# First attention of a two-layer trunk: a head's four score-reading operations emitted with nothing between them

## The chip, the cores and the metric

The kernel runs on one core of a Trainium2 chip. The metric is the device time of one execution in microseconds (us), as the median over several runs. The profile is of one further execution of the same program; its times are counted from the first instruction of its span.

## The reference: what is computed

The reference is a small decoder trunk over one sequence of 256 tokens of width 1024, in float32. It has two layers, and each layer does: a half-step SwiGLU feed-forward, an attention, a second half-step feed-forward. Every sub-layer is fed by an RMS norm that is modulated by a shift and a scale, and its result is added through a gate; shifts, scales and gates are one vector each, made from the conditioning vector `c`:

```python
c_act = silu(c)
mod = c_act @ ada_w[layer] + ada_b[layer]          # 9 vectors of 1024: sh1, sc1, g1, ... sh3, sc3, g3
h = rms_norm(x, g1n) * (1 + sc1) + sh1;  x = x + 0.5 * g1 * swiglu(h, w_in, w_out)
h = rms_norm(x, g2n) * (1 + sc2) + sh2;  x = x + g2 * attention(h)
h = rms_norm(x, g3n) * (1 + sc3) + sh3;  x = x + 0.5 * g3 * swiglu(h, w_in2, w_out2)
```

The first layer's attention is differential: 8 heads, each with two query/key maps of 64 and values of 128 wide. For each of the two maps the logits `q k^T / 8 + bias` go through a causal softmax, the second map's weights are subtracted with a factor lambda, the result multiplies the values, and an RMS norm and an output projection follow. The second layer's attention is an ordinary one with a decay by forget gates. A final RMS norm ends the trunk.

## The kernel before

**Matrix products.** Activations are held as a sum of two lower-precision parts (`HH`, `HL`: 128 features by up to 258 columns for each of eight k), and so are weights (`wh`, `wl`). A product is three matmuls on TensorE: wh·HH, wl·HH, wh·HL (`mm3`, L418). The weights of the whole program are one stream of pieces of mostly 128x1024. Each piece is loaded by SP into one of six buffers (`raw`), rounded by ScalarE (ACT) into its high part `wh` (`cp_part`, L306), and VectorE (DVE) subtracts to get its low half `wl` (`sub_part`, L318). A `raw` buffer comes free, and the next load is issued, when its low half has been made.

**Modulation sums.** The vectors `mod` are not made by TensorE. They are 160 sums on DVE (`ada_block`, L198): each multiplies a 128x1024 tile of `ada_w` with `c_act` and adds it up along the row, which gives 128 numbers of one vector. One load by SP (1 MB) brings a tile for two sums; three such tiles are held, and the load of tile u+3 is issued when the second sum of tile u is done (`ada_dma`, L185). The sums are numbered here from 0: the gate of the first attention and the scale and shift of the feed-forward behind it need the sums up to number 63.

**What sets the order on an engine.** Every instruction of ACT, DVE, TensorE (PE) and SP stays in the order in which the program emits it. While it emits, the program keeps a rough clock for each engine (class `InOrder`, L55). When an instruction would have to wait by these clocks, `fill_dve` (L372) first emits other work ahead of it: low halves, or modulation sums, if the clock of DVE is more than 0.6 us ahead of the operand and a credit allows the sum. The same work is emitted from `bg` (L386), called after each group of matmuls. `plain(f, ...)` (L133) switches the filling off for the time of `f`. In the mode "fill", which starts when the first attention has only its output projection left, `bg` and `fill_dve` emit no sums at all. What is not yet done when a vector is needed is emitted on the spot by `need` (L236), one sum after the other:

```python
def need(*ms):
    while ada_done[0] < 2 * max(ada_at[m] for m in ms):
        credit[0] -= 1
        dve.plainly(ada_block)
```

**The first attention** (`attention_a`, L1050). The heads run as a software pipeline. While PE projects the query/key and value matrices (`v_proj`, `pair_proj`) or multiplies by the output matrix, `group(t)` (L1161) emits for head t the score matmuls and their reading, for head t-1 the transposed weights, for head t-2 the product with the values, for head t-3 the transposed output. The reading is `exps` (L1084): for two maps and two halves of the queries, DVE takes scores plus bias and the row's bound (`nl<-s,g`, 128x128 and 128x256), and ACT takes the exponential. `combine` (L1103) then scales and subtracts the two maps on DVE, `inv_rms` has a power on POOL, and `out_split` makes the high and low part of the head's output (`oh`, `ol`). Until the change, only head 7's reading is emitted through `plain`.

**Behind it.** `OutProj.finish` (L872) emits the last quarter of the output projection into four PSUM banks (`pw`), calls `need` for the gate of this attention and the scale and shift of the next feed-forward, writes the shift into two extra columns of `HH` and `HL` (`shift_cols`, L432), and then, for each of the eight 128-feature blocks n, `x_update` (L438): the residual `x` on DVE, its scaled copy into `HH` on ACT, a square on ACT, the remainder into `HL` on DVE, and a running sum of squares (`acc`) on POOL, the last on DVE. The next feed-forward (`ffn`, kind "late", L632) starts its first product on these not yet normalised columns (`lg`, `lu`), k by k; after k = 2 it issues the matmul of the sum of squares (`psn`, L464), from which the norm is made; its second product (`pg1`) uses the normalised columns.

Of the kernel before, what the change touches and what calls it, by code (L numbers as in the profile page):

```python
# [22 lines left out]
AH = 8  # L23
# [81 lines left out]
def trunk(ctx, tc, a, out):  # L105
# [22 lines left out]
    def bbank(name):  # L128
        return pp.tile([P, 512], F32, tag="tb", name=name)
# [3 lines left out]
    def plain(f, *args):  # L133

        r = []
        act.plainly(lambda: dve.plainly(lambda: r.append(f(*args))))
        return r[0]
# [912 lines left out]
    def attention_a():  # L1050
# [24 lines left out]
        def scores(hd):  # L1075
            sb = [sbank(f"s{hd}_{m}") for m in range(2)]
            for qt, (c0, w) in enumerate(QT):
                for m in range(2):
                    rows = slice(m * HD, m * HD + HD)
                    mm(sb[m][:, c0:c0 + w], qk[hd][rows, qt * P:qt * P + P], qk[hd][rows, 256:256 + w],  # L1080
                       start=True, stop=True)
            return sb

        def exps(hd, sb):  # L1084
            g = gs[hd]
            nl = []
            nm = kp.tile([P, 4], F32, tag="nm", name=f"nm{hd}")
            sm = kp.tile([P, 4], F32, tag="sm", name=f"sm{hd}")
            for m in range(2):
                s = sb[m]  # L1090
                n_ = cp_.tile([P, 384], F32, tag=f"hidh{4 + 2 * (hd % 2) + m}", name=f"nl{hd}_{m}")
                nl.append(n_)
                for qt, (c0, w) in enumerate(QT):
                    cc = 2 * m + qt
                    dve.tensor_tensor_reduce(
                        n_[:, c0:c0 + w], s[:, c0:c0 + w], g[:, S - w:], -0.125, BIG,
                        ALU.add, ALU.min, accum_out=nm[:, cc:cc + 1])
                    act.activation(n_[:, c0:c0 + w], n_[:, c0:c0 + w], AF.Exp,
                                   bias=nm[:, cc:cc + 1], scale=-1.0,
                                   accum_out=sm[:, cc:cc + 1])  # L1100
            st[hd], sms[hd] = nl, sm
# [15 lines left out]
        def weights_t(hd):  # L1117
            pw = abank(f"pw{hd}")
            for b in range(3):
                pe.transpose(pw[:, b * P:b * P + P], st[hd][:, b * P:b * P + P], ident)  # L1120
            return pw

        def values(hd, po):
            wt = st[hd]
            vs = slice((hd % 4) * P, (hd % 4) * P + P)
            v0, v1 = va[0][hd // 4][:, vs], va[1][hd // 4][:, vs]
            mm(po[:, 0:P], wt[:, 0:P], v0, start=True, stop=True)
            mm(po[:, P:2 * P], wt[:, P:2 * P], v0, start=True, stop=False)
            mm(po[:, P:2 * P], wt[:, 2 * P:3 * P], v1, start=False, stop=True)

        def squares(hd, po):
            on = kp.tile([P, 256], F32, tag="w512b", name=f"on{hd}")
            ss = kp.tile([P, 2], F32, tag="ss", name=f"ss{hd}")
            for qt in range(2):
                act.activation(on[:, qt * P:qt * P + P], po[:, qt * P:qt * P + P], AF.Square,
                               accum_out=ss[:, qt:qt + 1])
            st[hd] = (po, on, ss)

        def inv_rms(hd):
            ss = st[hd][2]  # L1140
            dve.tensor_scalar(ss, ss, 1.0 / P, EPS, op0=ALU.mult, op1=ALU.add)
            nc.gpsimd.tensor_tensor(ss, ss, half, op=ALU.pow)
            InOrder.ready[(ss.tensor.name, 0)] = dve.t + 1.0
# [8 lines left out]
        def out_t(hd, pz):  # L1152
            for qt in range(2):
                pe.transpose(pz[:, qt * P:qt * P + P], st[hd][:, qt * P:qt * P + P], ident)

        def out_split(hd, pz):
            oh, ol = o[hd]
            act.activation(oh, pz, AF.Identity, scale=subg)
            dve.scalar_tensor_tensor(ol, pz, subg, oh.bitcast(F32), op0=ALU.mult, op1=ALU.subtract)

        def group(t):  # L1161

            hs, hw, hv, ho = (h if 0 <= h < AH else None for h in (t, t - 1, t - 2, t - 3))
            bank = bbank(f"po{t}") if hv is not None or ho is not None else None
            sb = scores(hs) if hs is not None else None
            pw = weights_t(hw) if hw is not None else None
            if hv is not None:
                values(hv, bank[:, :256])
            if ho is not None:
                out_t(ho, bank[:, 256:])  # L1170
            if hw is not None:
                wt = cp_.tile([P, 384], F32, tag=f"hidh{8 + hw % 2}", name=f"wt{hw}")
                act.copy(wt, pw[:, :384])
                st[hw] = wt
            if hs is not None:
                plain(exps, hs, sb) if hs == AH - 1 else exps(hs, sb)
            if hv is not None:
                squares(hv, bank[:, :256])
                inv_rms(hv)
            if ho is not None:  # L1180
                plain(out_split, ho, bank[:, 256:]) if ho == AH - 1 else out_split(ho, bank[:, 256:])
# [17 lines left out]
        for i, _ in enumerate(v_proj("wv", va)):  # L1199
            run_laters()  # L1200
            if i in (3, 9):
                group(i // 6)
            if i in (5, 11):
                after(i // 6)
        for t in range(2, AH):
            qk.append(qk_tile(t))
            for i, _ in enumerate(pair_proj("wqk", qk[t], f"pqk{t}")):
                if t > 2 and i == 2:
                    group(t - 1)
                if t > 2 and i == 5:  # L1210
                    combine(t - 1)
                if t > 2 and i == 7:
                    scale_o(t - 3)
        step(4)
        group(AH - 1)
        for t, n in (AH - 1, 9), (AH, 6), (AH + 1, 3):
            step(6)
# [362 lines left out]
```

## Time and profile before

| | us |
|---|---|
| median of 3 runs | 966.03 (965.13 to 966.9) |
| the profiled execution | 964.94 |
| its span, first to last instruction | 962.9 |

| engine | busy us | share of the span |
|---|---|---|
| PE | 954.6 | 99% |
| DVE | 821.1 | 85% |
| ACT | 556.9 | 58% |
| POOL | 72.5 | 8% |

PE carries the three matmuls for each product, and its share is near the whole span. A busy PE is not the same as a PE at its peak, since the ends of matmuls are modelled; idle time of PE, however, is seen as such. In the profile almost every operation carries line 100, because a helper records it; the tiles (`ada`, `wl`, `nl`, `pw`, `lg`, ...) tell them apart. A row of the timeline gives start, duration, engine, operation, output and inputs.

The first attention lies between 193 and 301 us of the span, the feed-forward behind it starts at 301.

### The profile page before, as it was taken

How to read it: one execution, taken by the hardware profiler on the slowest of the kernel's cores; microseconds unless marked ns; L12 is line 12 of the kernel's file. 1: busy time of each engine (PE TensorE's matmuls, PEld its weight loads, DVE VectorE, ACT ScalarE, POOL GpSimd, SP SyncE). 2: the span in 40 equal slices, each digit the busy share in tenths (PEclk: the TensorE clock that was granted, in tenths of full speed). 3: DMA queues.
4: the chain of work that ended last, by engine and by line, in shares of the span. 5: the costliest groups of instructions: out<-in, count | busy, mean ns of one | idle time of the engine just before them, and what ended most of it. 6: DMA issues, size and time to landing. Idle time of an engine off the chain costs nothing.

```text
span 962.9 us, 20487 instructions
## 1 busy us (share of the span) xinstructions
PE 954.6 (99%) x8090; PEld 930.9 (97%) x8090; DVE 821.1 (85%) x1369; ACT 556.9 (58%) x908; POOL 72.5 (8%) x119
## 2 busy tenths in 40 slices
PE   9999999999999999999999999999999999999997
PEld 7999999988999999999997999999998899999997
DVE  8989988889999999878889988889988799555575
ACT  6575655566777645455577554445568766554432
POOL 0000001100112000000000000000044014200000
PEclk9999999999999999999999999999999999999999
DMA  9998989968767699878959899988995437987641
GB/s 369 413 368 311 376 314 317 372 216 292 280 214 255 211 389 375 293 280 315 330 198 369 303 340 339 343 294 317 317 323 163 118 128 219 268 166 253 192 148 44
DMA packets 69661, 267.89 MB, mean 278 GB/s; under 512 B 9572, under 2 KB 10413, under 8 KB 59454
## 3 DMA queue, kind: packets, MB, share of 16 engines
q1 hardware_dynamic: 66060, 259.35, 76.7%
q0 software_dynamic: 3072, 6.92, 2.5%
q8 instruction: 63, 1.03, 0.4%
q10 hardware_dynamic: 434, 0.33, 0.1%
q14 instruction: 32, 0.26, 0.1%
HBM read 264.42 MB, written 2.66 MB: 277 GB/s over the span
## 4 chain that ended last, share of the span: by engine, by line
PE 92%; DVE 4%; ACT 2%; issue 2%; DMA 0%; POOL 0%; SPq 0%; DVEq 0%; ACTq 0%; POOLq 0%
PE po L100 25%; PE pg L100 22%; PE pu L100 21%; PE pv L100 5%; PE pf L100 5%; PE lp L100 4%; PE pw L100 3%; DVE wl L100 1%; PE lq L100 1%; PE lu L100 1%; PE lg L100 1%; PE pk L100 1%; DVE nl L100 1%; PE wb L100 1%; ACT nl L100 1%
## 5 line engine op out<-in xcount | busy, mean ns | idle before, releaser
L100 ACT CAST wh<-raw 128x1024 fp32r<-128x1024 f32 (+1 forms) x360 | 347.8, 975 | 212.2 <-PE pu L100 87.2
L100 DVE TENSOR_TENSOR wl<-raw,wh 128x1024 fp32r<-128x1024 f32 (+1 forms) x360 | 400.1, 1126 | 76.1 <-ACT sg L100 25.0
L100 DVE CUSTOM_DVE_ANT_0 ada<-ada,cact,vecs 128x1024 f32<-128x1024 f32 x144 | 182.6, 1277 | 0.0
L100 PE MATMUL pg<-HH,wl 128*128 128x256 f32 x608 | 167.9, 276 | 0.0
L100 PE MATMUL pu<-HH,wh 128*128 128x256 f32 x608 | 167.9, 276 | 0.0
L100 PE MATMUL pg<-HH,wh 128*128 128x256 f32 x608 | 167.9, 276 | 0.0
L100 PE MATMUL pu<-HL,wh 128*128 128x256 f32 x608 | 167.9, 276 | 0.0
L100 PE MATMUL pg<-HL,wh 128*128 128x256 f32 x608 | 167.9, 276 | 0.0
L100 PE MATMUL pu<-HH,wl 128*128 128x256 f32 x608 | 167.9, 276 | 0.0
L100 PE MATMUL po<-hidh,wh 128*128 128x256 f32 x528 | 145.7, 276 | 0.0
L100 PE MATMUL po<-hidh,wl 128*128 128x256 f32 x528 | 145.7, 276 | 0.0
L100 PE MATMUL po<-hidl,wh 128*128 128x256 f32 x528 | 145.7, 276 | 0.0
L100 PEld LDWEIGHTS pg<-HH,wl 128*128 128x128 f32 x608 | 114.1, 188 | 0.0
L100 PEld LDWEIGHTS pg<-HH,wh 128*128 128x128 f32 x608 | 114.1, 188 | 0.0
L100 PEld LDWEIGHTS pg<-HL,wh 128*128 128x128 f32 x608 | 114.2, 188 | 0.0
L100 PEld LDWEIGHTS pu<-HH,wh 128*128 128x128 f32 x608 | 114.2, 188 | 0.0
L100 PEld LDWEIGHTS pu<-HL,wh 128*128 128x128 f32 x608 | 114.1, 188 | 0.0
L100 PEld LDWEIGHTS pu<-HH,wl 128*128 128x128 f32 x608 | 114.1, 188 | 0.0
L100 PEld LDWEIGHTS po<-hidl,wh 128*128 128x128 f32 x528 | 99.1, 188 | 0.0
L100 PEld LDWEIGHTS po<-hidh,wl 128*128 128x128 f32 x528 | 99.1, 188 | 0.0
L100 PEld LDWEIGHTS po<-hidh,wh 128*128 128x128 f32 x528 | 99.1, 188 | 0.0
L100 ACT CAST hidh<-hf 128x512 fp32r<-128x512 f32 x44 | 27.3, 621 | 45.4 <-DVE hf L100 45.4
(244 smaller groups left out, 1878.0 us busy)
## 6 DMA issues: line engine op xcount, KB each, us to landing
raw<-in_win SPq DMA_DIRECT2D x176, 512.0 KB, 5.8
ada<-in_ada SPq DMA_DIRECT2D x79, 1024.0 KB, 7.3
raw<-in_wout SPq DMA_DIRECT2D x48, 384.0 KB, 5.5
raw<-in_wout SPq DMA_DIRECT2D x48, 320.0 KB, 5.2
raw<-in_wqk SPq DMA_DIRECT2D x16, 512.0 KB, 5.2
raw<-in_wo SPq DMA_DIRECT2D x16, 512.0 KB, 5.2
raw<-in_wlast SPq DMA_DIRECT2D x16, 512.0 KB, 4.3
raw<-in_wv SPq DMA_DIRECT2D x8, 512.0 KB, 9.0
```

The source lines that it names most:

```text
L100: return self.tc.keep_in_program_order(f(*args, **kw))
```

## The change

In `group`, the reading of a head's scores is emitted through `plain` for every head, where it was for head 7 alone:

```diff
--- before.py
+++ after.py
@@ -1173,7 +1173,7 @@
                 act.copy(wt, pw[:, :384])
                 st[hw] = wt
             if hs is not None:
-                plain(exps, hs, sb) if hs == AH - 1 else exps(hs, sb)
+                plain(exps, hs, sb)
             if hv is not None:
                 squares(hv, bank[:, :256])
                 inv_rms(hv)
```

No instruction is added or taken away; PE, POOL and, in the attention, ACT have the same order as before. DVE and SP have another. Three places follow. In the rows, `ISA ada,modall` is a modulation sum, and the number behind a name tells buffers apart.

The first is DVE at the scores of head 3, before the change:

```order
L100 TENSOR_TENSOR wl_3235<-raw_2996,wh_3177 128x1024
L100 ISA nl3_0_3234,nm3_3232<-s3_0_3215,g3_2964 128x128
L100 ISA nm3_3232 128x1
L100 ISA ada_3005,modall_91<-ada_3005,cact_89,vecs_75 128x1024
L100 ISA modall_91 128x1
L100 SCALAR_TENSOR_TENSOR modall_91<-modall_91,vecs_75 128x4
L100 ISA nl3_0_3234,nm3_3232<-s3_0_3215,g3_2964 128x256
```

and with it:

```order
L100 TENSOR_TENSOR wl_3192<-raw_2977,wh_3078 128x1024
L100 ISA nl3_0_3227,nm3_3225<-s3_0_3208,g3_2960 128x128
L100 ISA nm3_3225 128x1
L100 ISA nl3_0_3227,nm3_3225<-s3_0_3208,g3_2960 128x256
L100 ISA nm3_3225 128x1
L100 ISA nl3_1_3232,nm3_3225<-s3_1_3209,g3_2960 128x128
```

The sum between the first and the second score operation is gone; a sum that stood behind the fourth is gone too. Over heads 1 to 6 the attention loses eight sums on DVE between its scores and the end of its pipeline, and one low half for each of the heads 4 to 6 moves from behind the first score operation to behind the fourth.

The second is DVE in `finish`, where the eight sums come back through `need`. Before the change, from the last head's `ol`:

```order
L100 SCALAR_TENSOR_TENSOR ol3_2603<-po10_3896,small_90,oh3_2599 128x256
L100 ISA ada_3483,modall_91<-ada_3483,cact_89,vecs_75 128x1024
L100 ISA modall_91 128x1
L100 TENSOR_TENSOR HL_93<-modall_91,HH_92 128x8x2
L100 SCALAR_TENSOR_TENSOR x_76<-pw0_3644,modall_91,x_76 128x256
L100 TENSOR_TENSOR wl_3934<-raw_3659,wh_3863 128x1024
L100 SCALAR_TENSOR_TENSOR x_76<-pw1_3645,modall_91,x_76 128x256
```

and with it (rows that read the 128 numbers out, `modall 128x1`, and the first of two sums of a tile are left out):

```order
L100 SCALAR_TENSOR_TENSOR ol3_2603<-po10_3879,small_90,oh3_2599 128x256
L100 ISA ada_3060,modall_91<-ada_3060,cact_89,vecs_75 128x1024
...
L100 ISA ada_3793,modall_91<-ada_3793,cact_89,vecs_75 128x1024
...
L100 ISA ada_3822,modall_91<-ada_3822,cact_89,vecs_75 128x1024
...
L100 ISA ada_3886,modall_91<-ada_3886,cact_89,vecs_75 128x1024
...
L100 ISA ada_3890,modall_91<-ada_3890,cact_89,vecs_75 128x1024
L100 ISA modall_91 128x1
L100 TENSOR_TENSOR HL_93<-modall_91,HH_92 128x8x2
L100 SCALAR_TENSOR_TENSOR x_76<-pw0_3627,modall_91,x_76 128x256
L100 SCALAR_TENSOR_TENSOR x_76<-pw1_3628,modall_91,x_76 128x256
```

One sum stood between `ol3` and the first `x_update`; now it is nine, on five tiles: the second sum of one (number 55) and two each of the next four (56 to 63). On SP the loads that follow these sums stand as five 1 MB loads in a row, where there was one. The low half that stood between the first two `x` operations is not there any more.

The third is where that low half went: DVE behind the running sum of squares, with the change.

```order
L100 TENSOR_TENSOR acc_3962<-acc_3962,sq7_4023 128x256
L100 TENSOR_TENSOR wl_4033<-raw_3642,wh_3846 128x1024
L100 TENSOR_TENSOR wl_4070<-raw_3685,wh_3919 128x1024
L100 TENSOR_TENSOR wl_4080<-raw_3745,wh_4064 128x1024
L100 SCALAR_TENSOR_TENSOR ra_4092<-psn_4087,eps_83,r0_4089 128x256
```

and PE at k = 2 of the feed-forward's first product, with the change:

```order
L100 MATMUL lu1_4032<-HL_93,wh_3798 128x258
L100 MATMUL lg0_4029<-HH_92,wh_3846 128x258
L100 MATMUL lg0_4029<-HH_92,wl_4033 128x258
L100 MATMUL lg0_4029<-HL_93,wh_3846 128x258
L100 MATMUL lg1_4030<-HH_92,wh_3846 128x258
```

The low half `wl_4033` that k = 2 and 3 use is the one that was `wl_3934` before, between the first two `x` operations; now it is made behind all eight `x_update` and the last `acc`.

## The prediction

> **What bounds the kernel now.** I read the page's first part, then the windows over the attention, then PE's waits, then the chain of waits around the end of the attention.
>
> ```profile
> PE 954.6 (99%) x8090; PEld 930.9 (97%) x8090; DVE 821.1 (85%) x1369; ACT 556.9 (58%) x908; POOL 72.5 (8%) x119
> 250.00:300.00 50.00, 49.74 (x431) 47.64 (x430) 46.13 (x119) 39.62 (x116) 7.38 (x12) 1.00 0.71 244
> PEld po L100 <- ACT on L100: 0.2, 1, 0.2
> ```
>
> PE is idle for only 8.3 of 962.9 us. In the second row (window, its length, then busy time of PE, PEld, DVE, ACT, POOL, then granted clock, DMA share, GB/s) it stands still for 0.26 us in the 50 us that hold most of the attention, and the third row says where: one wait on the head's normalised output. So DVE's order inside the attention costs PE a quarter of a microsecond. The chain of waits shows that wait and what follows (start, duration, what):
>
> ```profile
> 291.40 0.63 ACT on L100 x2
> 292.07 0.44 PE po L100 x2
> 292.51 8.48 PE pw L100 x72
> 301.00 0.71 PE lg L100 x6
> ```
>
> From 292.51 PE has 8.5 us of output projection that needs nothing new, and at 301.00 it must have the first updated columns. DVE in that stretch, from the timeline:
>
> ```profile
> 285.41 1.28 DVE L100 CUSTOM_DVE_ANT_0 ada<-ada,cact,vecs 128x1024 f32<-128x1024 f32 x1
> 290.23 0.08 DVE L100 DVE_READ_ACCUMULATOR2_ANT modall<- 128x1 f32 x1
> 293.20 0.48 DVE L100 SCALAR_TENSOR_TENSOR ol<-po,small,oh 128x256 fp32r<-128x256 f32 x1
> 293.60 1.27 DVE L100 CUSTOM_DVE_ANT_0 ada<-ada,cact,vecs 128x1024 f32<-128x1024 f32 x1
> 294.80 0.08 DVE L100 DVE_READ_ACCUMULATOR2_ANT modall<- 128x1 f32 x1
> 295.25 0.48 DVE L100 SCALAR_TENSOR_TENSOR x<-pw,modall,x 128x256 f32<-128x256 f32 x1
> 295.64 1.22 DVE L100 TENSOR_TENSOR wl<-raw,wh 128x1024 fp32r<-128x1024 f32 x1
> 296.77 0.48 DVE L100 SCALAR_TENSOR_TENSOR x<-pw,modall,x 128x256 f32<-128x256 f32 x1
> 297.17 0.48 DVE L100 SCALAR_TENSOR_TENSOR HL<-x,modall,HH 128x256 fp32r<-128x256 f32 x1
> 304.04 0.41 DVE L100 TENSOR_TENSOR acc<-acc,sq 128x256 f32<-128x256 f32 x1
> 304.37 3.48 DVE L100 TENSOR_TENSOR wl<-raw,wh 128x1024 fp32r<-128x1024 f32 x3
> ```
>
> The first `HL` is ready at 297.65, 3.35 us before PE wants it, and the sum of squares at 304.45, 0.7 us before its matmul (PE, same view; the first row is the first use of the low half of k = 2):
>
> ```profile
> 303.83 0.28 PE L100 MATMUL lg<-HH,wl 128*128 128x258 f32 x1
> 305.15 0.59 PE L100 MATMUL psn<-acc,ones 128*128 128x256 f32 x2
> ```
>
> These two slacks are what eight more sums on DVE must fit into.
>
> **The change part by part.** The sum is made for the start of `psn`, 305.15 now; behind it the same operations follow in nearly the same order.
>
> (a) *Eight sums move behind `ol`.* Four sums fill 285.41 to 290.23, so one takes 1.205 us, and eight 9.64 us. Before, they lay in the attention, where PE had other work; now they stand in front of `x_update`, and the ACT copies, the squares, POOL's sums and PE's first product all queue behind.
>
> (b) *Their tiles.* SP's loads of `ada_w` here, and the time to landing of such loads (both 286.72 loads, then the one at 294.91, then all of 200 to 300 us):
>
> ```profile
> 286.72 2.74 SPq L100 DMA_DIRECT2D ada<-in_ada  x2
> 294.91 0.33 SPq L100 DMA_DIRECT2D ada<-in_ada  x1
> ada<-in_ada SPq DMA_DIRECT2D x1, 1024.0 KB, 6.4
> ada<-in_ada SPq DMA_DIRECT2D x1, 1024.0 KB, 6.5
> ada<-in_ada SPq DMA_DIRECT2D x1, 1024.0 KB, 7.1
> DMA to landing us min/median/max: 5.1/7.2/7.8
> ```
>
> Three tiles are held, so the sums on the first three of the five tiles run without a wait, to 293.60 + 5 x 1.205 = 299.62. The fourth tile's load is issued when the first sum is done, at 294.91, where now the last one is. With 6.4 us it lands at 301.3: a wait of 1.7. The fifth is issued two sums later, 297.3, and lands with 6.5 at 303.8, when the fourth tile's sums end at 303.7: 0.1. Together 1.8 us. With 5.1 it is 0.4, with 7.8 it is 3.1. I take 1.8, since the loads at 286.7 are two in a row like these.
>
> [...]
>
> (c) *From the last sum to `psn`.* Before: 305.15 - 294.80 = 10.35 us. After: 0.45 to the first `x` (294.80 to 295.25); from there to the end of `acc` 304.37 - 295.25 = 9.12, less the 1.13 of the low half that is no longer within (295.64 to 296.77), 7.99; then that low half, 1.2; then what k = 2 has left when it arrives, 305.15 - 303.83 = 1.32. That is 10.96, so 0.6 us more. The low half is on the path now because PE's k = 2 needs it and it stands behind `acc`: before, it was ready 7 us early. Bounds: 0, if the row of updates closes up better, and 1.5, if ACT's copies and POOL's sums of about 0.9 us each, which now lack the gap, hold the updates back:
>
> ```profile
> 298.18 0.85 POOL L456 TENSOR_TENSOR acc<-sq,sq 128x256 f32<-128x256 f32 x1 [6.82 <-ACT sq L100]
> ```
>
> (d) *The attention.* Without the sums the wait at 292.07 goes, -0.25 us, and the row of nine starts that much earlier. It can't be more: PE has no other idle time there. The three moved low halves have their matmuls several us later, and the sum ahead of them is gone, so they cost nothing; if one did come late, it would be by at most its 1.2 us.
>
> (e) *The clock.* PE's idle time is now far over 3 us: from 301 until the first two banks, which the first product takes over, are read out by the fifth and the sixth `x`:
>
> ```profile
> 299.24 0.47 DVE L100 SCALAR_TENSOR_TENSOR x<-pw,modall,x 128x256 f32<-128x256 f32 x1
> 300.51 0.47 DVE L100 SCALAR_TENSOR_TENSOR x<-pw,modall,x 128x256 f32<-128x256 f32 x1
> ```
>
> By (a), (b) and (d) the first `x` moves from 295.25 to 306.4; now the two end 4.46 and 5.73 us behind it, and 3.3 and 4.6 without the low half between, so at 309.8 and 311.0. The rows at the kernel's end show what idleness does, and the warm-up matmuls at its start what work before full speed costs:
>
> ```profile
> 956.00:957.00 1.00, 0.21 (x2) 0.01 (x1) 0.71 (x2) 0.00 (x0) 0.00 (x0) 1.00 0.69 241
> 959.00:960.00 1.00, 0.00 (x0) 0.00 (x0) 0.00 (x0) 0.00 (x0) 0.00 (x0) 0.88 0.38 151
> 960.00:961.00 1.00, 0.00 (x0) 0.00 (x0) 0.00 (x0) 0.00 (x0) 0.00 (x0) 0.50 0.95 369
> 1.13 1.65 PE L100 MATMUL warm<-ones 128*128 128x128 f32 x6 [1.13 <-DVE ones L100]
> 6.25 1.63 PE L100 MATMUL warm<-ones 128*128 128x128 f32 x8
> 8.75 1.58 PE L100 MATMUL warm<-ones 128*128 128x128 f32 x12
> ```
>
> PE's last work ends at 956.21; a granted clock of 0.88 in the slice from 959 means that it fell to a half at 959.76, 3.55 us later. At the start six matmuls take as long as twelve do 7.6 us on. So PE comes back at half speed. The 21 matmuls of k = 0 and 1 that are left once both banks are free take 2.5 us at 0.12 us each and 5.1 at half speed. So k = 1 ends near 316.1, against 306.4 + 7.99 + 1.2 = 315.6 for the low half: 0.5 us. If the clock is back before then, 0; if k = 2 runs at half speed too, 0.5 + 1.5 = 2.0. I take 0.5.
>
> [...]
>
> Sum: 9.64 + 1.8 + 0.6 - 0.25 + 0.5 = **12.3 us**. The profiled execution would go from 964.94 (span 962.9) to 977.2; the median of the runs shown is 966.03, 1.1 above that execution, and with the same 12.3 it gives **978.3 us**. The rest of the program has the same work; later sums stand a place or two further on, under a PE that is busy throughout, and cost nothing. If the cover is thin there, it would be just behind, where the low halves of the second and third product come up to 1 us later against slacks of about 1 us: 0 to 0.8.
>
> **The rivals.**
>
> *Partly hidden.* The sums fill the slack first: 3.35 us at the first `HL`. Then 9.64 - 3.35 = 6.3 us, and 972.3. For it speaks that slack; against it that the sum of squares has only 0.7 and the low half of k = 2 none. It would need PE to reach `psn` with both in hand.
>
> *Hidden.* The 8.5 us of output projection cover the sums: 966. Against it: one sum, the updates and `acc` already use 293.6 to 304.45 of the time up to 305.15.
>
> *Faster.* The chain of waits leaves PE in the middle of the attention and comes back at 292:
>
> ```profile
> 229.73 4.12 PE pqk L100 x37
> 233.85 1.20 DVE ada L100
> 284.96 0.69 POOL ss L1142
> ```
>
> If these DVE operations were what PE waits for, the eight sums taken out would end the attention 9.64 us sooner and the stall behind would start from there: 956.4 at best, if the sums' return were covered. It would decide if PE's idle time in the attention were of that size; it is 0.26 us of 50.
>
> *A long low clock.* If PE stays at half speed as long as at the start of the kernel, from 1.13 to past 6.25, where eight matmuls still take what twelve do later, so some 6 us, half of that, 3.0, is lost in place of 0.5: 980.8. [...] For it speaks that start; against it that PE waits for DVE in part of that time anyway.
>
> **How the numbers follow.** My forecast has 0.80, the long clock 0.08, partly hidden 0.06, hidden 0.03, faster 0.03. The low end of the forecast is 9.64 + 0.4 + 0 - 0.25 + 0 = 9.8, or 975.8; the high end 9.64 + 3.1 + 1.5 - 0.25 + 2.0 + 0.8 = 16.8, or 982.8. I give 974 to 983.5, which leaves out the three cases on the low side. A change of 0.2%, 1.9 us, is about what a measurement of this kernel can tell from none. Slower by more than that: 0.94; within: 0.03; faster: 0.03.
>
> **What would show it.** In the profile of the changed kernel: nine sums in a row on DVE from about 293.3 to 306, with a pause of 1 to 2 us before the sixth; PE idle from about 300.8 for some 9 us, then a second pause before k = 2, put down to `wl`; a granted clock under 1.00 in the slices near 305 to 316; `psn` near 317.5; the 0.2 us wait at 292 gone. It is wrong if PE's idle time before `lg` is under 4 us, if the sixth sum doesn't wait, or if the slices behind show a clock of 1.00 throughout.

## The result and the profile after

| | before | after |
|---|---|---|
| median | 965.58 (4 runs, 964.48 to 966.9) | 978.96 (4 runs, 977.9 to 979.93) |
| ratio | | 1.0130, 95% interval 1.0113 to 1.0147 |
| the profiled execution | 964.94 | 979.93 |
| its span | 962.9 | 978.0 |

The changed kernel is slower by 13.4 us, 1.3%. The forecast was 978.3, with 974 to 983.5 as its range.

The first part of the page after:

```profile
PE 959.8 (98%) x8090; PEld 936.0 (96%) x8090; DVE 822.4 (84%) x1369; ACT 557.2 (57%) x908; POOL 72.8 (7%) x119
```

The instruction counts are those of before. DVE is busy 1.3 us longer and PE 5.2 us, but the span is 15.1 us longer: most of the time went into waiting. (Most of PE's 5.2 us is that the same matmuls run slower at the start and behind a stall; both are shown below.) PE's waits between 60 and 345 us (who, tile, line, released by: total, times, longest) show where:

```profile
PE pw L100 <- DVE x L100: 9.1, 1, 9.1
PE lg L100 <- DVE wl L100: 1.2, 1, 1.2
```

The wait of 0.2 us for the head's output is gone, and two new ones stand behind the attention. DVE's timeline there (start, duration, operation, and in brackets the idle time ahead with what ended it); the first sum, the fifth, the sixth and the ninth are shown:

```profile
295.12 0.48 DVE L100 SCALAR_TENSOR_TENSOR ol<-po,small,oh 128x256 fp32r<-128x256 f32 x1
295.51 1.27 DVE L100 CUSTOM_DVE_ANT_0 ada<-ada,cact,vecs 128x1024 f32<-128x1024 f32 x1
...
300.33 1.28 DVE L100 CUSTOM_DVE_ANT_0 ada<-ada,cact,vecs 128x1024 f32<-128x1024 f32 x1
303.13 1.28 DVE L100 CUSTOM_DVE_ANT_0 ada<-ada,cact,vecs 128x1024 f32<-128x1024 f32 x1 [1.51 <-DMA ada<-in_ada]
...
306.94 0.16 DVE L100 SCALAR_TENSOR_TENSOR modall<-modall,vecs 128x4 f32<-128x4 f32 x1
307.02 1.28 DVE L100 CUSTOM_DVE_ANT_0 ada<-ada,cact,vecs 128x1024 f32<-128x1024 f32 x1
308.67 0.87 DVE L100 SCALAR_TENSOR_TENSOR x<-pw,modall,x 128x256 f32<-128x256 f32 x2
...
316.80 0.41 DVE L100 TENSOR_TENSOR acc<-acc,sq 128x256 f32<-128x256 f32 x1
317.14 3.48 DVE L100 TENSOR_TENSOR wl<-raw,wh 128x1024 fp32r<-128x1024 f32 x3
```

Nine sums stand in a row between the last `ol` and the first `x`, with a pause of 1.51 us before the sixth, and the low halves stand behind `acc`. PE in the same stretch:

```profile
299.81 0.28 PE L100 MATMUL pw<-ol,wh 128*128 128x256 f32 x1
309.20 0.58 PE L100 MATMUL pw<-oh,wh 128*128 128x256 f32 x1 [9.11 <-DVE x L100]
309.58 0.41 PE L100 MATMUL pw<-oh,wl 128*128 128x256 f32 x1
...
318.40 0.39 PE L100 MATMUL lg<-HH,wl 128*128 128x258 f32 x1 [1.20 <-DVE wl L100]
319.83 0.59 PE L100 MATMUL psn<-acc,ones 128*128 128x256 f32 x2
```

PE stops not at `lg` but inside the output projection: the fifth block (n = 4) writes the other half of the bank from which the first x update reads (`out(n)` takes bank n % 4), and it waits for that update. 24 of the 72 matmuls are still to come then. The windows (length, busy time of PE, PEld, DVE, ACT, POOL, then granted clock, DMA share, GB/s) give the clock:

```profile
303.00:304.00 1.00, 0.00 (x0) 0.00 (x0) 0.87 (x1) 0.00 (x0) 0.00 (x0) 0.60 1.05 442
309.00:313.00 4.00, 3.80 (x18) 3.80 (x19) 3.40 (x9) 3.52 (x10) 1.49 (x2) 0.50 0.88 348
313.00:314.00 1.00, 1.00 (x8) 1.00 (x8) 1.00 (x3) 0.90 (x3) 0.86 (x2) 0.78 0.06 25
```

A mean of 0.60 over the slice from 303 means that the clock fell to a half at 303.2, 3.1 us after PE's last matmul ended at 300.09, and a mean of 0.78 from 313 that it came back at 313.44, 4.2 us after PE's restart at 309.20.

**Part of the 15.1 us is not the change.** The last matmul of the very first product, before and then after:

```profile
56.90 0.28 PE L100 MATMUL pf<-HL,wh 128*128 128x256 f32 x1
```

```profile
9.95 2.91 PE L100 MATMUL warm<-ones 128*128 128x128 f32 x12
59.26 0.28 PE L100 MATMUL pf<-HL,wh 128*128 128x256 f32 x1
```

The programs are alike up to there, but this execution is 2.36 us later: its warm-up matmuls at 9.95 still ran slowly (2.91 us for the twelve that took 1.58 before). The granted clock of the profile is 1.00 over these first 15 us in both executions, so only the durations tell it. Over all profiled executions here the first `pf` starts anywhere between 12.0 and 14.6 us, whatever the kernel. So all that follows is counted from the last `pf`:

| from, to | before | after | difference |
|---|---|---|---|
| last `pf` to last `ol` (the attention and all before) | 236.30 | 235.86 | -0.44 |
| last `ol` to first `x` (the sums) | 2.05 | 13.55 | +11.50 |
| first `x` to `psn` | 9.90 | 11.16 | +1.26 |
| `psn` to the end | 657.75 | 658.17 | +0.42 |
| together | 906.00 | 918.74 | +12.74 |

12.74 is what the two traces give for the change; the medians, with their own start-ups, give 13.4.

### The profile page after: what moved, and what is told of

It reads as the page before. It is cut to its first block, busy times and chain, and to the rows that moved or that the text cites. A ratio compares the mean times of both kernels' runs of the same rounds, so it can differ in the third digit from the quotient of the medians.

```text
span 978.0 us, 20486 instructions
## 1 busy us (share of the span) xinstructions
PE 959.8 (98%) x8090; PEld 936.0 (96%) x8090; DVE 822.4 (84%) x1369; ACT 557.2 (57%) x908; POOL 72.8 (7%) x119
## 4 chain that ended last, share of the span: by engine, by line
PE 96%; DVE 2%; ACT 1%; DMA 1%; issue 0%; POOL 0%; DVEq 0%; ACTq 0%
PE po L100 25%; PE pg L100 21%; PE pu L100 21%; PE pv L100 5%; PE pf L100 5%; PE lp L100 4%; PE pqk L100 3%; PE pw L100 3%; PE lq L100 1%; PE pk L100 1%; DVE ada L100 1%; PE lg L100 1%; PE lu L100 1%; PE wb L100 1%; PE sb L100 1%; PE s L100 1%
## 5 line engine op out<-in xcount | busy, mean ns | idle before, releaser
L100 PE MATMUL po<-wh,hidh 128*128 128x256 f32 x176 | 48.6, 276 | 0.0
```

Of the source, the lines that this page charges most:

```text
L100: return self.tc.keep_in_program_order(f(*args, **kw))
```

## The experiments

The theory: reading the scores without anything between costs nothing; the cost is that sums end up in a row behind the last `ol` (the burst), each paid in full, and the low half behind `acc` once. The first rival: the reading order itself holds PE up. In the table "sums" is the number between the last `ol` and the first `x`, and the next columns are those above, each from one profiled execution; a few tenths between two rows can be the execution (the last row has the attention of the kernel before, and 0.34 us less up to `ol`).

| run | sums | `pf` to `ol` | `ol` to `x` | `x` to `psn` | `psn` to end | together | median, us | ratio to before (95%) |
|---|---|---|---|---|---|---|---|---|
| before | 1 | 236.30 | 2.05 | 9.90 | 657.75 | 906.00 | | |
| the change | 9 | 235.86 | 13.55 | 11.16 | 658.17 | 918.74 | 978.96 | 1.0130 (1.0113 to 1.0147) |
| burst alone | 9 | 235.50 | 12.19 | 11.15 | 658.00 | 916.84 | 976.52 | 1.0105 (1.0089 to 1.0121) |
| order alone | 1 | 243.64 | 2.05 | 9.84 | 657.83 | 913.36 | 972.97 | 1.0066 (1.0048 to 1.0084) |
| five left | 5 | 235.66 | 7.06 | 11.13 | 657.70 | 911.55 | 971.43 | 1.0054 (1.0039 to 1.0070) |
| low half in the pause | 9 | 235.86 | 14.39 | 9.61 | 659.85 | 919.71 | 979.42 | 1.0132 (1.0116 to 1.0149) |
| order, spread | 1 | 240.01 | 2.05 | 9.85 | 657.71 | 909.62 | 970.32 | 1.0044 (1.0028 to 1.0060) |
| clock kept, too long | 9 | 235.86 | 14.74 | 11.45 | 672.14 | 934.19 | 994.21 | 1.0289 (1.0268 to 1.0311) |
| heads 4 to 7 | 4 | 235.62 | 5.86 | 11.16 | 657.76 | 910.40 | 970.73 | 1.0050 (1.0030 to 1.0070) |
| none left | 0 | 241.68 | 1.62 | 10.37 | 658.01 | 911.68 | 970.58 | 1.0048 (1.0025 to 1.0070) |
| clock kept | 9 | 235.87 | 14.55 | 11.15 | 657.72 | 919.29 | 978.55 | 1.0116 (1.0096 to 1.0135) |
| same work behind | 1 | 236.86 | 3.19 | 11.00 | 658.83 | 909.88 | 971.22 | 1.0045 (1.0027 to 1.0063) |
| six moved | 1 | 235.86 | 2.04 | 9.94 | 658.12 | 905.96 | 965.40 | 0.9997 (0.9985 to 1.0009) |
| low half late | 1 | 235.96 | 2.04 | 13.23 | 658.83 | 910.06 | 970.90 | 1.0047 (1.0030 to 1.0065) |

The medians of the kernel before beside these runs were between 965.4 and 966.9.

### The burst alone, and fewer sums in it

The kernel before, with its reading order, but a cap on the number of sums in the first attention:

```diff
-if mode[0] == "run" and credit[0] >= 1.0 and (full >= FULL or not splittable()):
+if mode[0] == "run" and credit[0] >= 1.0 and ada_done[0] < cap[0] and (full >= FULL or not splittable()):
...
     pace[0] = PACE[1]
+    cap[0] = 55
     op, rest = attention_a()
```

> The heads' scores are read as in the kernel before, with sums between the four operations, but in the first attention no sum is emitted beyond number 54, so that nine are left for the spot behind the last `ol`, as in the changed kernel. Theory (the nine sums behind `ol` are the whole cost): 978 to 979 us, +12.5 to +13.4, with the sixth sum waiting about 1.5 us for its tile, the x update about 13 us later than before and a wait for `wl` of about 1.2 us before `psn`. Rival (the order in which the scores are read costs the time, by what it does to PE inside the attention): 965 to 967 us, as before. A mixture would lie between, and split the 13 us.

Without any change to the reading the time is 976.52 us, 9.8 over the kernel before and below the 978 to 979 that was expected; the traces give 10.84 of the 12.74 us. `x` to `psn` is that of the changed kernel to 0.01 us. The difference that is left to the changed kernel, 1.9 us, lies mostly between `ol` and `x`: the sixth sum hardly waits for its tile (0.15 us: it starts at 300.11, the fifth was read out at 299.96). The `ada` loads in this stretch land sooner; here, and then in the changed kernel:

```profile
DMA to landing us min/median/max: 4.7/4.8/5.0
```

```profile
DMA to landing us min/median/max: 5.7/6.2/6.3
```

In the changed kernel two such loads and two weight loads had been issued from 288.6 to 295.6, just ahead; here the last weight load was issued at 292.7. That this is the reason was not tried: the run with the clock kept (below) issues the same four loads as long ahead as the changed kernel, and its `ada` loads have a median of 7.2 us.

With the cap at 59:

> As the run with the burst alone, but sums up to number 58 are allowed, so that five are left behind the last `ol` where nine are in the changed kernel and one is before. The three tiles held are enough for five, so none should wait for a load. Theory (every sum moved there is paid in full, no slack takes any of it): four more sums at 1.205 us are 4.8, the low half behind `acc` adds the 1.2 to 1.3 that it adds in the changed kernel: +6.1, 971.7 us. Rival (PE's cover of the output projection takes the first part: its fifth block would wait for the first x update only from 2.4 us of delay on): 4.8 - 2.4 = +2.4, 968 us.

The traces give 911.55 - 906.00 = +5.55 us, the medians +4.7. The waits of this run:

```profile
PE pw L100 <- DVE x L100: 2.5, 1, 2.5
PE lg L100 <- DVE wl L100: 1.7, 1, 1.7
```

The rival is half right on the wait and wrong on the time. The first x update comes 5.0 us later behind the last `ol`, PE waits 2.5 for it, so there is indeed a cover of 2.5 us at the fifth block. But `psn` is 5.6 us later all the same, because behind the first `x` it is DVE's own chain that leads to it, and that chain has no cover.

The change in part, for half of the heads:

```diff
-plain(exps, hs, sb)
+plain(exps, hs, sb) if hs >= 4 else exps(hs, sb)
```

> The change for heads 4 to 7 only; heads 0 to 3 are read as before. Four sums are left behind the last `ol`, three more than before, all on tiles that are held. Theory (each sum left there is paid in full, and the low half behind `acc` once): 3 x 1.205 + 1.25 - 0.3 = +4.6, 970.5 us. Rival (cover takes the first part, as for a price by the first wait of PE at 2.4 us): +1.2, 967 us.

970.73 us, where the theory had 970.5; that is +5.4 against the median before in the same series, and +4.4 by the traces. Between `ol` and `x` the runs with 1, 4, 5 and 9 sums (the last without a wait for a tile worth naming) have 2.05, 5.86, 7.06 and 12.19 us: 1.25 to 1.27 per further sum, from the first to the last. And `x` to `psn` is 11.13 to 11.16 with 4, 5 and 9 sums, 1.25 more than before, whether 3 or 8 sums were moved.

### The order alone

This took five tries. The first emits sums right behind a head's four operations, as many as the credit allows:

```diff
 plain(exps, hs, sb)
+while credit[0] >= 1.0 and ada_done[0] < cap[0]:
+    credit[0] -= 1.0
+    dve.plainly(ada_block)
```

> The scores are read as in the changed kernel, four operations with nothing between them, but sums that the credit allows are emitted right behind the four, up to number 62, so that only one is left behind the last `ol`, as before. Theory (the nine sums are the whole cost): 965.2 us, the time before less the 0.25 to 0.4 us that the attention gained in the changed kernel's trace, within 964.5 to 966.5. Rival (the reading order costs): up to 979 us. Second rival (sums in rows of two to five ahead of a head's `rs` hold up its weights): 966 to 970 us, with waits of PE for `nl`, `wt` or `on` between 230 and 292 us.

972.97 us: the second rival, and more than it had. The loss is ahead of `ol`, 243.64 against 236.30. Behind head 0's four operations stand six sums, from 214.73 to 221.98, the first and the last of them here:

```profile
214.73 1.28 DVE L100 CUSTOM_DVE_ANT_0 ada<-ada,cact,vecs 128x1024 f32<-128x1024 f32 x1
220.77 1.28 DVE L100 CUSTOM_DVE_ANT_0 ada<-ada,cact,vecs 128x1024 f32<-128x1024 f32 x1
```

and PE waits for what is queued behind them, head 0's weights and the low halves of the value projection:

```profile
223.17 0.33 PE L100 MATMUL pw<-tri,nl 128*128 128x128 f32 x1 [1.23 <-DVE nl L100]
223.96 0.44 PE L100 MATMUL pw<-tri,nl 128*128 128x128 f32 x2 [0.45 <-DVE nl L100]
225.09 0.50 PE L100 MATMUL pv<-wl,HH 128*128 128x512 f32 x1 [0.47 <-DVE wl L100]
231.59 0.50 PE L100 MATMUL pv<-wl,HH 128*128 128x512 f32 x1 [1.90 <-DVE wl L100]
```

The granted clock is low there besides, with a mean of 0.66 from 225 to 230 us: the `pv` matmuls that start from 225.96 to 228.52 take 0.63 us each, where they took 0.39 up to 220.46.

The second has at most two sums in that place (`for _ in range(2)` with the same condition):

> As the run with the order alone, but at most two sums behind a head's four operations (there it was six in a row behind head 0's), one sum left behind the last `ol`, as before. If the row of six made that run 6 us slower (it held back head 0's weights and the low halves of the value projection), this one stands where the kernel before stands, 965 to 967 us, with no wait of PE over 0.5 us between 205 and 300 us. If reading the scores with nothing between costs time itself, it stays near 973 us.

970.32 us lies between the two times that were expected, 965 to 967 and near 973. The trace does not put it down to the reading order: up to 260 us PE doesn't wait at all, and then twice for a low half:

```profile
PE pqk L100 <- DVE wl L100: 2.3, 1, 2.3
PE pw L100 <- DVE wl L100: 1.6, 1, 1.6
```

Here two sums stand behind heads 4 to 6 where the kernel before has one low half and one sum. The third, with number 63 too done ahead, has the same fault:

> The changed reading, at most two sums behind each head's four operations, and number 63 too is done there, so that none is left behind the last `ol`. The x update starts 1.2 us earlier than in the kernel before. Theory (PE is busy throughout from 292 us on in the kernel before, so a DVE that is earlier gains nothing): 965 to 966.5 us, no more than 0.3 us under the run with one sum left. Rival (the updates set the start of the feed-forward even before the change): 1.2 us less, 964 to 965.

It has two waits of 2.3 and 1.8 us for low halves as well, so its 970.58 says nothing on whether the last sum costs anything before the change; that stays open. The fourth try puts the low halves back, by a table for each head, and four sums ahead of head 7's last `ol`:

```diff
+for e in {1: "s"}.get(hs, ""):
+    if e == "s":
+        credit[0] -= 1.0
+        dve.plainly(ada_block)
+    else:
+        sub_part()
 plain(exps, hs, sb)
+for e in {1: "ss", 2: "ss", 3: "ss", 4: "ws", 5: "ws", 6: "ws"}.get(hs, ""):
...
 after(t)
+if t == AH:
+    for _ in range(4):
+        credit[0] -= 1.0
+        dve.plainly(ada_block)
 step(n)
```

> The scores are read as in the changed kernel, and the sums and low halves that the kernel before has between a head's four operations and right behind them are emitted right behind the four, in the same numbers: two sums each for heads 1 to 3, a low half and a sum each for heads 4 to 6, and four sums ahead of head 7's last `ol`s, so that one is left. In the two runs before this one with sums behind the four, sums took the place of low halves, and PE waited 2.3 and 1.6 us for those. Theory (neither the reading order nor the place within a head matters, only that low halves are in time and that no sums are left behind `ol`): 964.5 to 966.5 us, as the kernel before, and no wait of PE over 0.5 us between 205 and 310 us. Rival (four operations with nothing between cost time themselves, 5 us as in those two runs): 969 to 971 us.

The time is the rival's, 971.22, but PE is busy throughout from 205 to 290 us, over all eight readings. What it loses (3.9 us in this trace, of an execution of 968.62 us, among the fastest of its ten), it loses behind them, in waits around the fillers ahead of head 7's last `ol`, among which stands one low half more than before:

```profile
PE po L100 <- ACT on L100: 1.1, 1, 1.1
PE pw L100 <- DVE wl L100: 0.7, 1, 0.7
PE lg L100 <- DVE x L100: 0.6, 1, 0.6
```

So the order of everything else had to be held fixed. The last try replays DVE's order of the kernel before in the first attention, operation by operation. With R for an operation of the attention, s for a sum and w for a low half, it is, from head 1's reading to head 4's:

```
before      sRsRRRsRRRRRRwwswwsswwRsRRRsRRRRRRRwwRsRRRsRRRRRRRRwRwRRRsRRRRRRRR
six moved   sRRRRssRRRRRRwwswwsswwRRRRssRRRRRRRwwRRRRssRRRRRRRRwRRRRwsRRRRRRRR
```

> The three runs with sums behind the four operations also changed where low halves and the last sums stand. Here the order of every engine is that of the kernel before but for DVE, and on DVE six instructions alone are moved: the one sum (heads 1 to 3) or the one low half (heads 4 to 6) that stands between a head's first and second score operation goes right behind the fourth, as the changed reading has it. One sum is left behind the last `ol`. Theory (reading the scores with nothing between costs nothing): as the kernel before within 0.2%, 965 to 968 us by the runs of this series (before: 965.4 to 966.9), and `psn` 248.2 to 248.7 us behind the last `pf`, with no wait of PE over 0.5 us between 205 and 310 us. Rival (it costs time itself, 4 to 5 us, as the last run's total would have it): 970 to 972 us.

965.40 us beside 965.9, a ratio of 0.9997 (0.9985 to 1.0009), and no wait of PE between 205 and 310 us. `psn` comes 247.84 us behind the last `pf`, 0.4 sooner than expected and than before, all of it ahead of `ol`; that much lies between executions (see (d) below). Reading a head's scores with nothing between costs nothing, and gains nothing that can be told. What the change costs is where the displaced sums end up.

### The low half behind `acc`

In the changed kernel, the low half for k = 2 is made in the pause before the sixth sum:

```diff
+while ada_done[0] < 60:
+    dve.plainly(ada_block)
+sub_part()
 need(gate, *nxt)
 shift_cols(nxt)
```

> The changed kernel with one edit: the low half that k = 2 of the first product needs is made between the fifth and the sixth of the nine sums, where DVE waits 1.5 us for a tile. Theory (that low half behind `acc` is on the path to `psn`, at 1.2 us): the wait for `wl` before `psn` goes, DVE is no later at the x update, and k = 2 follows k = 1 on PE: 1.2 us less than the changed kernel, 977.7. Rival (the updates and squares set `psn`, the low half only fills what PE would wait anyway): 978.9, the same as the changed kernel.

The step is right and the gain is not there. `x` to `psn` falls from 11.16 to 9.61, and `psn` comes 0.7 us earlier; `ol` to `x` grows by 0.84, since the pause was longer than in the changed kernel's trace (1.20 us were left of it behind the low half). But behind `psn` 1.7 us are lost again, 1.4 of them in two waits for other low halves (0.5 and 0.9 us). DVE has a fixed row of low halves to make in this stretch; it seems that a place for one is a place less for the next. By its time, 979.42 us, the rival has it.

The opposite edit, in the kernel before: the low half between the first and the second x update is kept back until the updates are done, and no sum is moved.

```diff
             shift_cols(nxt)
+            halt[0] = gate == (0, 5)
...
             f()
+            halt[0] = False
             done[0] += 1
...
-        while True:
+        while not halt[0]:
```

> The kernel before with one change: the low half that DVE makes between the first and the second x update is kept back until the updates are done, where the changed kernel has it, and no sum is moved. Theory (that place alone makes the way from the first x update to `psn` 11.15 us, as in every run with sums left behind, where it is 9.90 before): `psn` 1.2 to 1.3 us later, with a wait for `wl` ahead of it, and the time 1.2 to 1.5 us over the kernel before. Rival (the wait for `wl` only appears together with the burst, since PE is late enough here): `psn` within 0.3 us of the kernel before.

The wait for `wl` appears without any burst, so the place of the low half is enough for it. But it is 2.2 us long and the whole costs 3.3 at `psn`, where 1.25 were expected. Two things add to it. The x updates themselves take 1.0 us more than before (first `x` to the end of `acc`: 10.17 against 9.20), and 1.6 more than in the changed kernel (8.54), where no low half stands between them either; and behind the wait the clock falls:

```profile
309.20 0.39 PE L100 MATMUL lg<-HH,wl 128*128 128x258 f32 x1 [2.21 <-DVE wl L100]
311.07 1.05 PE L100 MATMUL psn<-acc,ones 128*128 128x256 f32 x2
```

```profile
310.00:311.00 1.00, 1.00 (x7) 1.00 (x6) 1.00 (x2) 0.09 (x1) 0.00 (x0) 0.51 0.81 188
313.00:314.00 1.00, 1.00 (x8) 1.00 (x8) 0.93 (x3) 0.94 (x1) 0.00 (x0) 0.78 0.86 287
```

The median is 5.0 us over the kernel before, but one of the six executions took 966.07 us, as little as the kernel before, and only one of the slower five has a trace. So this run shows that the wait comes from the low half's place, but not its price in the changed kernel; that is read from the runs with 4, 5 and 9 sums, where `x` to `psn` is 11.13 to 11.16.

### The clock

The changed kernel with matmuls of ones on ones, whose result nobody reads, ahead of the fifth block:

```diff
+                if n == 4:
+                    warm(64)
                 for kk in range(2):
                     mm3(self.out(n), blk(kk * D + n * P), self.o[6 + kk], False, kk == 1)
```

> The changed kernel with 64 matmuls of ones on ones emitted ahead of the fifth block of the output projection, about 8.4 us of work that nobody reads, so that TensorE is not idle while it waits for the first x update. Theory (the half clock is hidden, since k = 2 waits for its low half anyway): the 24 matmuls behind the stall run at full speed, the wait for `wl` grows by the 2.2 us that they save, `psn` starts where it starts in the changed kernel, and the time is 978.5 to 979.5 us. Rival (the low clock is on the path, as the term of 0.5 us in the prediction has it): 0.5 us less or more than that, up to 2.0, so 977 to 978.4.

This was mis-sized twice. The 64 took 14.45 us, longer than the wait, and they were emitted in the second attention's projection too, where they cost another 14 us (`psn` to the end: 672.14). Mended, with `n == 4 and gate == (0, 5)` and 40 of them:

> The run that kept the clock again, with its size mended: 40 matmuls of ones, in the first attention alone. In the run before, 64 took 14.45 us (0.226 each), 5 us longer than the wait, and they stood in the second attention's projection too. 40 should take 9.0 us of the wait of 9.1. Theory (the half clock is hidden): the 24 projection matmuls behind the stall take 2.8 us where they took 5.1, the granted clock stays at 1.00, but `psn` starts as late behind the last `ol` as in the changed kernel (24.7 us, within 0.2), with a wait for `wl` of about 3.4 us in place of 1.2: 978.5 to 979.5 us. Rival (the low clock is on the path): `psn` 0.5 us or more sooner behind `ol`, 977 to 978.4 us.

```profile
303.00:304.00 1.00, 1.00 (x11) 1.00 (x10) 1.00 (x3) 0.00 (x0) 0.00 (x0) 1.00 0.99 418
309.00:313.00 4.00, 3.40 (x25) 2.82 (x24) 3.79 (x9) 3.41 (x10) 2.33 (x3) 1.00 0.59 246
```

```profile
308.26 0.39 PE L100 MATMUL pw<-oh,wh 128*128 128x256 f32 x1 [1.19 <-DVE x L100]
317.46 0.39 PE L100 MATMUL lg<-HH,wl 128*128 128x258 f32 x1 [1.67 <-DVE wl L100]
318.88 0.59 PE L100 MATMUL psn<-acc,ones 128*128 128x256 f32 x2
```

The clock stays at 1.00 through the stretch, and `psn` comes 11.15 us behind the first `x`, where it is 11.16 with the half clock. The half clock costs nothing here: DVE's chain sets `psn`, and PE only waits less when it runs slower. The wait for `wl` is 1.67 us and not the expected 3.4, since PE waits 0.6 us for the updates at `lg` too. `psn` comes 25.70 us behind `ol`, not 24.7: `ol` to `x` is 1.0 us longer than in the changed kernel, because the sixth sum waits 2.52 us for its tile in this execution; that is the load, not the clock.

## Why the prediction was right

Point by point, by the parts of its sum (12.3 us; the traces give 12.7):

- **(a) Eight sums at 1.205 us**: right, 9.64. Some 0.35 us between them had no term: reading one out takes up to 0.08 us, such a readout stands uncovered before the sixth, the eighth and the ninth sum, and a small operation on four numbers, done ahead before (at 290.35), stands in front of the ninth now (306.94).
- **(b) The tiles**: 1.8 foretold, 1.51 measured, at the sixth sum as foretold; the fifth tile added nothing. In other runs with nine sums the same pause was 0.15 (burst alone), 2.41 (low half in the pause), 2.52 and 2.70 (clock kept), within the bounds of 0.4 to 3.1 but for the first, so the term came out near by some luck. The `ada` loads issued from 290 to 310 us took 4.7 to 5.0 us to land in the run with the burst alone, 5.7 to 6.3 in the changed kernel and 4.7 to 7.3, with a median of 7.2, in the mended run with the clock kept; what sets that time was not shown.
- **(c) From the last sum to `psn`**: 0.6 foretold. The measured difference between first `x` and `psn` is 1.26: the row of updates closed up by 0.66 and not by the 1.13 of the low half, since with two `x` in a row at its head the first `HL` waits 0.40 us for ACT's copy; the low half behind `acc` then took 1.19, and the rest of k = 2 took 1.43. Its mechanism is right, its size was half.
- **(d) The attention**: -0.25 foretold, -0.44 measured, but not by the step that was given. The wait at 292 was read from the weight loads (PEld); PE itself stands still there for 0.05 us. Most of its 0.26 us is elsewhere, a wait for ACT's `qk`:

```profile
275.13 0.93 PE L100 MATMUL s<-qk 64*128 64x128 f32 x8 [0.20 <-ACT qk L100]
```

Neither wait shows in the run with the low half late, whose attention is that of the kernel before; it is 0.34 us shorter up to `ol`, and the run with six moved, whose sums are all still in the attention, is 0.44 shorter. So a gain of this size can lie between two executions of the same order, no run shows that taking the sums out gains anything, and that the sign was right was luck.
- **(e) The clock**: 0.5 foretold, nothing found. The clock did fall, 3.1 us behind PE's last matmul where 3.55 was taken, and come back, but the prediction had PE's pause at `lg`, behind the whole output projection, and k = 1 as late as the low half. The pause is ahead of the fifth block of that projection. Its length, some 9 us, was right by chance: the rule by which it was worked out (two banks free) was not the one that held. In the end k = 2 waited 1.20 us for the low half, and that wait took in whatever the half clock cost ahead of it. From the first `x` to `psn`, the runs with and without a warm PE agree to 0.01 us.
- **Behind `psn`**: nothing in the sum, 0 to 0.8 as bounds, +0.42 measured. The changed kernel with the clock kept has 657.72 us there, no more than the kernel before (657.75), so this can be the execution.

So the mechanism that carries the sum, eight sums paid in full ahead of the updates, a tile that comes late and a low half on the path, is the right one; that the total is so near is in part luck. (c) too small by 0.66 and (e) too large by 0.5 make up for each other: the two together were 1.1 in the sum and are 1.26 in the trace.

Of the rivals, *partly hidden* rested on a slack of 3.35 us at the first `HL`. There is a cover (2.5 us at the fifth block, by the run with five sums left), but it is cover for PE's first wait and not for `psn`, which hangs on DVE's chain. *Hidden* falls with it. *Faster* had the attention end 9.64 us sooner without the eight sums; it ends 0.44 sooner in the changed kernel and 0.80 in the run with the burst alone. *A long low clock* did not come about: the clock was back 4.2 us after the restart, and it would not have mattered. Of the three signs that would have shown the prediction wrong, a sixth sum that doesn't wait and a clock of 1.00 throughout didn't occur. The third, under 4 us of idle time of PE before `lg`, didn't if all idle time ahead of `lg` counts (9.11 us); at `lg` itself PE doesn't wait at all (it starts at 314.02 right behind the projection), and that is the fault of (e). `psn` stood at 319.83 and not near 317.5, but 2.36 us of that is the start-up of this execution.

## What to carry to other kernels

Work that fills gaps has a due time. When it is pushed out of one place, ask where it comes up again: here eight sums left a stretch in which PE hardly waited and came up as one block on the path, each at its full price. A cover that shows in the first wait of the busy engine (2.5 us) is no cover for a result further on, if another engine's own chain leads there. And to test an order of operations alone, hold the order of everything else fixed: four runs that put the same sums elsewhere lost 4 to 7 us for other reasons, and their totals alone would have told the wrong story.

## What the runs showed of the hardware that was not expected

**The half clock came after much shorter pauses too, and not each time.** The prediction took it from the end of the kernel, 3.55 us after PE's last work; here it came with pauses of 2.2 to 2.5 us. The same pause, at the same place, in two runs (the one with sums spread, then the one with none left, and the windows of the latter):

```profile
262.78 0.39 PE L100 MATMUL pqk<-HH,wl 128*128 128x256 f32 x1 [2.27 <-DVE wl L100]
```

```profile
260.82 0.58 PE L100 MATMUL pqk<-HH,wl 128*128 128x256 f32 x1 [2.27 <-DVE wl L100]
```

```profile
260.00:261.00 1.00, 0.17 (x1) 0.18 (x2) 1.00 (x2) 0.52 (x1) 0.00 (x0) 0.80 1.02 434
263.00:264.00 1.00, 1.00 (x7) 1.00 (x7) 1.00 (x2) 0.00 (x0) 0.00 (x0) 0.50 0.92 320
264.00:265.00 1.00, 1.00 (x12) 0.84 (x11) 0.18 (x1) 0.00 (x0) 0.00 (x0) 0.99 1.08 356
```

In the first the granted clock stays at 1.00 (the mean from 260 to 265 us); in the second it is a half from 260.6 to 264.0, 3.4 us. In the run with the low half late, a pause of 2.21 us is followed by a half clock that starts only at about 310.0, 0.8 us after PE's restart, and lasts until 313.4 (means of 0.51 and 0.78 in the slices from 310 and 313, above); in the run with five left, one of 2.49 us by a half clock from 302.6 to 306.0 (0.81 in the slice from 302, 0.98 in that from 306). So in three runs the half clock lasted 3.4 us, and a pause of 2.27 us had two outcomes; what decides between them no run shows. Nor was it shown why the first `pf` starts anywhere between 12.0 and 14.6 us.

**An `HL` on DVE that started while a sum of POOL ran ended 0.27 to 0.29 us behind it, and took up to twice its time.** In the run with the low half late, `HL` on DVE and `acc` on POOL start at nearly the same moment:

```profile
300.15 1.04 DVE L100 SCALAR_TENSOR_TENSOR HL<-x,modall,HH 128x256 fp32r<-128x256 f32 x1
301.51 0.95 DVE L100 SCALAR_TENSOR_TENSOR HL<-x,modall,HH 128x256 fp32r<-128x256 f32 x1
```

```profile
300.17 0.74 POOL L457 TENSOR_TENSOR acc<-sq,sq 128x256 f32<-128x256 f32 x1 [6.21 <-ACT sq L100]
301.44 0.74 POOL L457 TENSOR_TENSOR acc<-acc,sq 128x256 f32<-128x256 f32 x1 [0.53 <-ACT sq L100]
```

Both `HL` end 0.28 us behind POOL's sum. So do the other four `HL` that meet such a sum in this run (0.28 to 0.29 us behind; the six take 0.83 to 1.04 us), and those of the kernel before and of the changed one that start while a sum runs (0.27 to 0.29), where the two overlap less: there `HL` takes 0.56 to 0.80 us, and 0.48 where it meets no sum. It goes the other way for the second `HL` of these two kernels, which starts 0.22 and 0.26 us ahead of POOL's first sum: it takes 0.48 us, and that sum 0.85 and 0.81, where the sums of the run with the low half late take 0.73 to 0.74. Yet in that run's first pair, where `HL` is the first by 0.02 us, it is `HL` that is long. The six `HL` take 5.54 us together, and 3.71 in the changed kernel; that difference of 1.8 us would account for the updates of this run, which are 1.6 us longer, but it was not tried apart.
